# Low halves of the mixer's weight blocks: accumulating transfers in place of VectorE subtractions

## The chip, the core and the metric

The kernel runs on one core of a Trainium2 chip. The core has a matrix engine (TensorE), a vector engine (VectorE), a scalar engine (ScalarE) and a general engine (GpSimd), which work in parallel, each through its own queue of instructions in order; SyncE only issues transfers here. In the profile they are PE (its weight loads PEld), DVE, ACT, POOL and SP. Sixteen DMA engines carry the transfers. The metric is the time of the whole program on the device, in microseconds (us).

## The reference

A decoder trunk of two layers over 512 tokens of width 1024, in float32. Each layer is a feed-forward part, a mixer and a second feed-forward part, each added to x. The mixer, cut to what matters:

```python
h = rms_norm(x, mix_norm[l])
proj = h @ w_in[l]                       # 1024 -> 2048: q, k, v, u of 512 each
q = apply_rope(q, cos, sin)              # 4 heads, two maps of 64 columns each
k = apply_rope(k, cos, sin)
o = diff_attention(q, k, v, lam)         # (softmax(Q1K1) - lam softmax(Q2K2)) V, causal
o = rms_norm(o, subln_gain[l]) * (1.0 - lam_init)
p = pool_mixer(u, pool_w[l], pool_scale[l])   # windows 2, 4, 8, 16, then a linear map
x = x + jnp.concatenate([o, p], axis=-1) @ w_out[l]
```

The feed-forward parts are `x + 0.5 * swiglu(h, w_gate, w_up, w_down)` with 2816 hidden columns.

## The kernel before, in words

**Three products for one.** TensorE multiplies in a rounded float32 form (fp32r in the profile). To keep float32 accuracy each operand is split into a high half, the rounded value, and a low half, the rest, and `mm3` issues three matmuls into one sum: high by high (L95), a second with the weights' high half (L96), and one with the weights' low half (L97). In the profile whi and wlo are the weights' halves. A block's first two products can start when whi is there; the third waits for wlo.

**How weights come in.** All weights are cut into blocks of 128 partitions by up to 1024 columns, 512 KB of float32. The lists `raws` and `plan`, filled before the work starts, hold them in the order of use. `block(src, by_dma)` (L102) adds a block and says how its halves are made. `weights()` hands out the next block, and first prepares blocks up to 4 ahead (`AHEAD`); their raw float32 form, wraw, is loaded by SyncE up to 3 blocks further ahead (`AHEAD_RAW`). There are 6 buffers for wraw and 5 each for whi and wlo, used in turn, so preparing a block also waits until the block five before it has been used for the last time.

**Two ways to make the halves.** Without `by_dma`, `split` copies wraw into whi on ScalarE (L143), which rounds it, and VectorE subtracts whi from wraw into wlo (L144). With `by_dma`, ScalarE writes minus wraw, rounded, into wlo (L164), GpSimd issues a transfer that reads the block from HBM a second time and adds it onto wlo (L165), and ScalarE copies wraw into whi (L166). Before the change the mixer's blocks go the first way; of the feed-forward parts, the gate and up blocks that are used as they are go the second.

**The mixer** (`mix`, L534) uses 26 blocks per layer: query and key projections of four heads, with the v projection (which holds 4 blocks at once), the two u projections and the pooling maps (a block of 256 columns each) among them, and the output projection. The attention of a head runs in four steps (`scores` L607, `turn` L632, `attend` L645) laid among those projections by tables (`S_AT`, `Y_AT`) and lags in counts of work items (`LAG_Q` and others). Scores need a head's qs, ks and kf (the queries' and keys' halves, L571 to L576); GpSimd clears half of kf first (L571).

**The output projection** (`out_work`, L730) has two halves. For its first four blocks it goes over the inner dimension in five stages, as the heads come ready, with all four blocks held from the first stage to the last; then the other four blocks, one after the other, each with all 24 matmuls at once (ps_wo in the profile). Below, out block 4 is the first of these, out block 5 the second. Each finished block is added to x, from which ScalarE and GpSimd start the next norm's sum of squares (ssum).

**Order.** A scheduler lays down the order on each engine ahead of time from a priority and its own estimate of times, so the order on every engine can change when operations are replaced.

Of the kernel before, what the change touches and what calls it, by code (L numbers as in the profile page):

```python
# [70 lines left out]
def trunk(ctx: ExitStack, tc: tile.TileContext, xT, gu1, dn1, win_qk, win_v, win_u, poolw, wout, gu2, dn2, small, lams, consts, outT):  # L71
# [30 lines left out]
    def block(src, by_dma=False):  # L102

        raws.append(src)
        plan.append(("block", len(raws) - 1, by_dma))

    def pair(gu):

        r = len(raws)
        raws.extend(gu[b] for b in (A11, A12, A21, A22))  # L110
        plan.append(("block", r, True))
        plan.append(("block", r + 1, True))
        plan.extend((("sums", r + 3), ("sum", "u1", r), ("sum", "u3", r), ("sum", "u4", r)))
        plan.append(("block", r + 3, True))

    def plain_pairs(first):
        return 2 if first else 1

    for l in range(L):
        for gu, dn in ((gu1, dn1), (gu2, dn2)):  # L120
            if gu is gu2:
                for c in range(2):
                    for i in range(2):
                        block(win_qk[l, c][:, i * 1024 : (i + 1) * 1024])
                for c in range(2):
                    for i in range(2):
                        block(win_v[l, c][:, i * 1024 : (i + 1) * 1024])
                for w in (win_qk[l, 2], win_u[l, 1], win_qk[l, 3], poolw[l, 1], win_u[l, 0], wout[l, 0], wout[l, 1], poolw[l, 0], wout[l, 2], wout[l, 3]):
                    for o in range(0, w.shape[-1], 1024):
                        block(w[:, o : min(o + 1024, w.shape[-1])])  # L130
            for hf, (q0, nq) in enumerate(PARTS):
                for q in range(q0, q0 + nq):
                    if q < plain_pairs(gu is gu1 and l == 0):
                        for b in range(4):
                            block(gu[l, q, b], bool(q or l or gu is gu2))
                    else:
                        pair(gu[l, q])
                for n in range(KD):
                    block(dn[hf][l, n])
# [808 lines left out]
```

## Time and profile before

| | us |
|---|---|
| median of three runs | 1763.78 |
| these runs | 1763.78, 1764.39, 1762.21 |
| profiled execution | 1762.4 |
| its span in the trace | 1760.4 |
| TensorE busy | 1729.1 (98%) |
| weight loads of TensorE busy | 1565.8 (89%) |
| VectorE busy | 1137.3 (65%) |
| ScalarE busy | 946.5 (54%) |
| GpSimd busy | 208.3 (12%) |

The span runs from the first to the last instruction of the trace; the execution's own time is 2.0 us longer. The mean granted clock of TensorE is 0.995 of full speed. The transfers move 240.66 MB, 137 GB/s on the mean: 169.18 MB in SyncE's queue (31.0% of the 16 engines' time) and 69.74 MB in GpSimd's (22.3%). The first mixer lies between about 358 and 530 us of the span, the second between 1227 and 1400 us. A busy share is a mean over the run; whether an engine holds up another is seen only in the waits and the timeline of a stretch. In a timeline a row gives the start, the duration, the line, the operation, and its output and inputs by the program's names; a bracket at its end gives the idle time of the engine before it and what ended that.

### The profile page before, as it was taken

To read this page: it belongs to the slowest core of one execution; us is meant where nothing else is said; L and a number is where in the kernel's file an instruction comes from. 1 tells how busy PE (TensorE), PEld (TensorE's weight loads), DVE (VectorE), ACT (ScalarE), POOL (GpSimd) and SP (SyncE) were. 2 spreads that over 40 slices of the span, in tenths; PEclk is the share of its full clock that TensorE was granted. 3 is DMA by queue.
4 is the path that set the end of the run, shared out by engine and by line. 5 is a ranking of instruction groups with operands and counts; after the bars stand their busy time and mean duration, and the time that the engine had idled before them with its cause. 6 is when DMAs were issued, how large, how long until landed. Compare 5 with 4: busy or idle time off the path is not lost.

```text
span 1760.4 us, 26873 instructions
## 1 busy us (share of the span) xinstructions
PE 1729.1 (98%) x10936; PEld 1565.8 (89%) x10936; DVE 1137.3 (65%) x1507; ACT 946.5 (54%) x1294; POOL 208.3 (12%) x215
## 2 busy tenths in 40 slices
PE   9999999999999999999999999999999999999997
PEld 7889989888788989989889899898887889899996
DVE  6855646577967746646587465466789596466463
ACT  7635626555566626626556265364555665374463
POOL 1001001120021001001210010012100400010001
PEclk9999999999999999999999999999999999999998
DMA  9555746522235747737757377374122647375551
GB/s 287 138 146 149 190 106 159 153 75 75 72 100 134 189 105 168 192 88 170 182 118 196 86 181 183 96 171 146 43 86 61 155 109 203 96 183 165 120 144 48
DMA packets 71723, 240.66 MB, mean 137 GB/s; under 512 B 7856, under 2 KB 12592, under 8 KB 71600
## 3 DMA queue, kind: packets, MB, share of 16 engines
q1 hardware_dynamic: 52304, 169.18, 31.0%
q0 software_dynamic: 19152, 69.74, 22.3%
q8 instruction: 85, 1.39, 0.3%
q14 instruction: 38, 0.31, 0.1%
q10 hardware_dynamic: 144, 0.03, 0.0%
HBM read 236.82 MB, written 2.10 MB: 136 GB/s over the span
## 4 chain that ended last, share of the span: by engine, by line
PE 87%; DVE 5%; DMA 3%; issue 2%; ACT 2%; SPq 1%; POOL 0%; POOLq 0%; DVEq 0%; ACTq 0%
PE ps_dn L96 9%; PE ps_dn L95 9%; PE ps_dn L97 9%; PE ps_a L97 8%; PE ps_a L96 8%; PE ps_a L95 8%; PE ps_c L95 4%; PE ps_c L96 4%; PE ps_c L97 4%; DMA wlo<-gu 2%; PE ps_g L97 2%; PE ps_g L95 2%; PE ps_g L96 2%; PE ps_pr L95 2%; PE ps_pr L97 2%
## 5 line engine op out<-in xcount | busy, mean ns | idle before, releaser
L143 ACT CAST whi<-wraw 128x1024 fp32r<-128x1024 f32 (+2 forms) x275 | 273.7, 997 | 417.2 <-PE ps_dn L96 146.4
L144 DVE TENSOR_TENSOR wlo<-wraw,whi 128x1024 fp32r<-128x1024 f32 (+2 forms) x275 | 317.8, 1157 | 110.0 <-ACT whi L143 108.3
L97 PE MATMUL ps_a<-bhi,wlo 128*128 128x256 f32 x1248 | 353.9, 284 | 2.5 <-DMA wlo<-gu 2.4
L95 PE MATMUL ps_a<-bhi,whi 128*128 128x256 f32 x1248 | 353.9, 284 | 0.5 <-ACT whi L166 0.5
L96 PE MATMUL ps_a<-blo,whi 128*128 128x256 f32 x1248 | 354.1, 284 | 0.0
L96 PE MATMUL ps_dn<-hlo,whi 128*128 128x512 f32 (+1 forms) x716 | 276.6, 386 | 0.0
L97 PE MATMUL ps_dn<-hhi,wlo 128*128 128x512 f32 (+1 forms) x716 | 276.1, 386 | 0.0
L95 PE MATMUL ps_dn<-hhi,whi 128*128 128x512 f32 (+1 forms) x716 | 275.7, 386 | 0.0
L165 POOL DMA_DIRECT2D wlo<-gu x133 | 116.0, 874 | 1113.9 <-ACT wlo L164 754.7
L97 PEld LDWEIGHTS ps_a<-bhi,wlo 128*128 128x128 f32 x1248 | 240.1, 192 | 2.9 <-DMA wlo<-gu 2.9
L95 PEld LDWEIGHTS ps_a<-bhi,whi 128*128 128x128 f32 x1248 | 240.0, 192 | 1.5 <-ACT whi L166 0.7
L96 PEld LDWEIGHTS ps_a<-blo,whi 128*128 128x128 f32 x1248 | 240.1, 192 | 0.8
L166 ACT CAST whi<-wraw 128x1024 fp32r<-128x1024 f32 x133 | 139.2, 1048 | 129.9 <-PE ps_dn L96 62.2
L507 DVE SCALAR_TENSOR_TENSOR x<-ps_dn,x 128x512 f32<-128x512 f32 (+1 forms) x98 | 66.7, 680 | 191.8 <-PE ps_dn L97 191.8
L95 PE MATMUL ps_c<-bhi,whi 128*128 128x256 f32 x624 | 176.9, 283 | 5.7 <-ACT bhi L143 5.7
L97 PE MATMUL ps_c<-bhi,wlo 128*128 128x256 f32 x624 | 176.8, 283 | 0.5 <-DVE wlo L144 0.5
L96 PE MATMUL ps_c<-blo,whi 128*128 128x256 f32 x624 | 176.7, 283 | 0.0
L96 PEld LDWEIGHTS ps_dn<-hlo,whi 128*128 128x128 f32 x716 | 134.5, 188 | 27.8 <-DVE hlo L144 1.4
L97 PEld LDWEIGHTS ps_dn<-hhi,wlo 128*128 128x128 f32 x716 | 134.5, 188 | 27.0
L95 PEld LDWEIGHTS ps_dn<-hhi,whi 128*128 128x128 f32 x716 | 134.5, 188 | 26.8
L164 ACT ACTIVATE wlo<-wraw 128x1024 fp32r<-128x1024 f32 x133 | 140.5, 1057 | 0.2 <-DMA wraw<-gu 0.2
L95 PEld LDWEIGHTS ps_c<-bhi,whi 128*128 128x128 f32 x624 | 119.9, 192 | 6.3 <-ACT bhi L143 6.3
(171 smaller groups left out, 3236.7 us busy)
## 6 DMA issues: line engine op xcount, KB each, us to landing
wraw<-gu SPq DMA_DIRECT2D x174, 512.0 KB, 3.7
wlo<-gu POOLq DMA_DIRECT2D x133, 512.0 KB, 7.2
wraw<-dn SPq DMA_DIRECT2D x64, 512.0 KB, 4.4
wraw<-dn SPq DMA_DIRECT2D x32, 384.0 KB, 3.3
wraw<-wqk SPq DMA_DIRECT2D x16, 512.0 KB, 3.7
wraw<-wo SPq DMA_DIRECT2D x16, 512.0 KB, 3.7
wraw<-wv SPq DMA_DIRECT2D x8, 512.0 KB, 3.6
wraw<-wu SPq DMA_DIRECT2D x8, 512.0 KB, 3.7
```

Of the source, the lines that this page charges most:

```text
L95: nc.tensor.matmul(out, a_hi, b_hi, start=start, stop=False, skip_group_check=more)
L96: nc.tensor.matmul(out, a_hi, b_lo, start=False, stop=False, skip_group_check=more)
L97: nc.tensor.matmul(out, a_lo, b_hi, start=False, stop=stop, skip_group_check=more)
L143: nc.scalar.copy(hi, raw)
L144: nc.vector.tensor_sub(lo, raw, hi.bitcast(F32))
L164: nc.scalar.mul(lo[:, :n], raw[:, :n], -1.0)
L165: nc.gpsimd.dma_start(lo[:, :n], src, accum_op=ALU.add)
L166: nc.scalar.copy(hi[:, :n], raw[:, :n])
L507: nc.vector.scalar_tensor_tensor(x[:, n, ts], ps[:, ts], -0.5, x[:, n, ts], ALU.mult, ALU.add)
```

## The change

The blocks of the mixer's weights are now added with `by_dma`:

```diff
@@ -121,13 +121,13 @@
             if gu is gu2:
                 for c in range(2):
                     for i in range(2):
-                        block(win_qk[l, c][:, i * 1024 : (i + 1) * 1024])
+                        block(win_qk[l, c][:, i * 1024 : (i + 1) * 1024], True)
                 for c in range(2):
                     for i in range(2):
-                        block(win_v[l, c][:, i * 1024 : (i + 1) * 1024])
+                        block(win_v[l, c][:, i * 1024 : (i + 1) * 1024], True)
                 for w in (win_qk[l, 2], win_u[l, 1], win_qk[l, 3], poolw[l, 1], win_u[l, 0], wout[l, 0], wout[l, 1], poolw[l, 0], wout[l, 2], wout[l, 3]):
                     for o in range(0, w.shape[-1], 1024):
-                        block(w[:, o : min(o + 1024, w.shape[-1])])
+                        block(w[:, o : min(o + 1024, w.shape[-1])], True)
```

So each of the mixer's 52 blocks (26 per layer) loses its subtraction on VectorE (L144) and gains a pass on ScalarE (L164) and a transfer issued by GpSimd (L165); its high half is made by L166 in place of L143. VectorE goes from 1353 rows of the program to 1299, ScalarE from 1093 to 1153, GpSimd from 67 to 119. TensorE and SyncE have the same instructions as before; TensorE's order differs in three places of each mixer.

On TensorE, the attention of the first mixer's third head, before (ps_o the attention products, ps_t the transposes of the weights a, ps_pr a projection):

```order
L653 MATMUL ps_o<-v,at 128x256
L95 MATMUL ps_pr<-xhi,whi 128x512
L96 MATMUL ps_pr<-xlo,whi 128x512
L97 MATMUL ps_pr<-xhi,wlo 128x512
L95 MATMUL ps_pr<-xhi,whi 128x512
L96 MATMUL ps_pr<-xlo,whi 128x512
L97 MATMUL ps_pr<-xhi,wlo 128x512
L638 MATMUL ps_t<-ident_r,a 128x128 x2
L654 MATMUL ps_o<-v,at 128x128
```

and now:

```order
L653 MATMUL ps_o<-v,at 128x256
L654 MATMUL ps_o<-v,at 128x128
L638 MATMUL ps_t<-ident_r,a 128x128 x2
L95 MATMUL ps_pr<-xhi,whi 128x512
L96 MATMUL ps_pr<-xlo,whi 128x512
L97 MATMUL ps_pr<-xhi,wlo 128x512
```

The second product (L654) and the two transposes (L638) now stand directly behind the first product, ahead of the six projection matmuls.

On ScalarE, the end of the first mixer before, where the high halves of the last blocks are copied (cath is the output projection's input, xhi the next norm's high half):

```order
L661 ACTIVATE junk,osum<-o,rl 128x128 x2
L676 ACTIVATE cath<-ps_ot,subg_3489 128x512
L143 CAST whi<-wraw 128x1024 x3
L240 ACTIVATE xhi<-x,sm 128x512
L245 ACTIVATE ssum<-x 128x512
```

and now:

```order
L676 ACTIVATE cath<-ps_ot,subg_3493 128x512
L166 CAST whi<-wraw 128x1024
L164 ACTIVATE wlo<-wraw 128x1024 x2
L166 CAST whi<-wraw 128x1024
L164 ACTIVATE wlo<-wraw 128x1024
L166 CAST whi<-wraw 128x1024
L240 ACTIVATE xhi<-x,sm 128x512
L245 ACTIVATE ssum<-x 128x512
```

Three copies in a row have become three copies and three negations, ahead of the next norm's work.

On GpSimd, the same mixer from the clearing of kf to its end, before:

```order
L571 MEMSET kf 64x512 x6
L298 TENSOR_TENSOR rT<-ms,nhalf 128x4 x2
L571 MEMSET kf 64x512 x2
L298 TENSOR_TENSOR rT<-ms,nhalf 128x4 x2
L251 TENSOR_TENSOR ssum<-ssum,sq 128x512
```

and now, from the last u projection's blocks on (wo are the output projection's blocks, pw a pooling map):

```order
L165 DMA wlo<-wu 128x1024
L571 MEMSET kf 64x512 x2
L298 TENSOR_TENSOR rT<-ms,nhalf 128x4 x2
L165 DMA wlo<-wu 128x1024
L165 DMA wlo<-wo 128x1024 x4
L571 MEMSET kf 64x512 x2
L165 DMA wlo<-pw 128x256
L298 TENSOR_TENSOR rT<-ms,nhalf 128x4
L165 DMA wlo<-wo 128x1024
L298 TENSOR_TENSOR rT<-ms,nhalf 128x4
L165 DMA wlo<-wo 128x1024 x3
```

The clearing of the last head's kf (L571) now stands behind five transfers, and the small operations of the head norms (L298) between transfers of wo.

## Rows read from the trace of the kernel before

**Rows 1.** Windows, the stretches of the mixers. Columns: us, then per engine; PEclk, DMA share, GB/s.
```profile
400.00:500.00 100.00, 95.50 (x502) 80.01 (x501) 84.97 (x190) 55.68 (x135) 5.10 (x7) 1.00 0.23 70
1300.00:1400.00 100.00, 96.07 (x474) 79.57 (x473) 80.53 (x163) 58.81 (x119) 17.06 (x16) 0.98 0.32 85
```

**Rows 2.** Waits of TensorE, whole run. Columns: us in total, times, longest us.
```profile
PE ps_c L95 <- ACT bhi L143: 5.7, 3, 1.9
PE ps_s L617 <- DVE qs L576: 5.0, 6, 1.2
PE ps_a L97 <- DMA wlo<-gu: 2.4, 1, 2.4
...
PE ps_t L638 <- DVE a L629: 2.0, 2, 1.0
...
PE ps_s L617 <- ACT p L621: 1.1, 3, 0.5
...
PE ps_o L654 <- DVE at L642: 0.4, 2, 0.2
```

**Rows 3.** Line L144. Columns: count: ns min/median/max, first to last start; forms.
```profile
L144 DVE TENSOR_TENSOR wlo<-wraw,whi x275: 406/1224/1237, 5.4 to 1727.0; 128x1024 fp32r<-128x1024 f32 x116, 128x768 fp32r<-128x768 f32 x16, 128x256 fp32r<-128x256 f32 x6
```

**Rows 4.** Timeline of VectorE, 446 to 455 us. Columns: start us, duration us.
```profile
446.92 1.21 DVE L144 TENSOR_TENSOR wlo<-wraw,whi 128x1024 fp32r<-128x1024 f32 x1
448.04 0.17 DVE L690 COPY win<-win 128x8 f32<-128x8 f32 x1
...
453.87 0.48 DVE L629 SCALAR_TENSOR_TENSOR a<-p,ratio 128x256 f32<-128x256 f32 x1
454.26 0.29 DVE L642 TENSOR_TENSOR at<-ps_t,at 128x128 fp32r<-128x128 f32 x1
```

**Rows 5.** Timeline of TensorE, 452 to 457 us.
```profile
452.85 0.33 PE L653 MATMUL ps_o<-v,at 128*128 128x256 f32 x1
...
454.50 0.41 PE L638 MATMUL ps_t<-ident_r,a 128*128 128x128 f32 x2
...
456.24 0.28 PE L653 MATMUL ps_o<-v,at 128*128 128x256 f32 x1
```

**Rows 6.** Timeline of ScalarE, 463 to 476 us.
```profile
472.51 0.63 ACT L575 ACTIVATE qs<-t 64x512 fp32r<-64x512 f32 x1
```

**Rows 7.** Timeline of TensorE, 469 to 475 us; brackets: idle before, releaser.
```profile
474.55 0.30 PE L617 MATMUL ps_s<-kf,qs 128*128 128x128 f32 x1 [1.21 <-DVE qs L576]
```

**Rows 8.** Timeline of ScalarE, 524 to 527 us.
```profile
525.29 1.05 ACT L164 ACTIVATE wlo<-wraw 128x1024 fp32r<-128x1024 f32 x1
```

**Rows 9.** Line L165, whole run.
```profile
L165 POOL DMA_DIRECT2D wlo<-gu x133: 849/872/1210, 21.0 to 1702.2; - x133
...
DMA to landing us min/median/max: 5.2/7.2/15.5
```

**Rows 10.** Timeline of ScalarE, 489 to 516 us.
```profile
507.49 2.95 ACT L143 CAST whi<-wraw 128x1024 fp32r<-128x1024 f32 x3 [1.51 <-PE ps_wo L96]
```

**Rows 11.** Timeline of TensorE, 507 to 514 us.
```profile
507.29 0.39 PE L97 MATMUL ps_wo<-cath,wlo 128*128 128x512 f32 x1
...
513.89 0.39 PE L97 MATMUL ps_wo<-cath,wlo 128*128 128x512 f32 x1
```

**Rows 12.** Timeline of GpSimd, 524 to 528 us.
```profile
526.64 0.87 POOL L165 DMA_DIRECT2D wlo<-gu  x1 [1.82 <-ACT wlo L164]
```

**Rows 13.** Line L165, from 508 to 545 us.
```profile
DMA to landing us min/median/max: 5.8/8.6/10.2
```

**Rows 14.** Windows, three short stretches.
```profile
558.00:568.00 10.00, 8.11 (x54) 7.79 (x53) 9.61 (x10) 8.17 (x11) 0.86 (x1) 0.83 0.44 132
908.00:918.00 10.00, 8.11 (x67) 7.82 (x66) 10.00 (x10) 9.55 (x13) 1.72 (x2) 1.00 0.46 130
1342.00:1349.00 7.00, 5.82 (x25) 5.13 (x26) 6.64 (x19) 3.41 (x13) 0.00 (x0) 0.76 0.27 81
```

**Rows 15.** Timeline of GpSimd, 415 to 505 us.
```profile
459.28 1.10 POOL L571 MEMSET kf<- 64x512 f32 x2 [15.35 <-PE ps_y L97]
```

## The prediction

> **What bounds the kernel now.** TensorE. Read first the stretches that hold the two mixers: TensorE is busy 95.5 and 96.1 of 100 us there, VectorE 85 and 81, ScalarE only 56 and 59 [rows 1]. VectorE is nowhere in the run as full as here, and one of its jobs is the subtraction that this change removes. Read next who makes TensorE wait [rows 2]: four of the rows belong to the mixers alone (ps_s, ps_t and ps_o are attention tiles): 5.0 us for the queries' low half (DVE L576), 2.0 for the attention weights (DVE L629), 1.1 for the exponentials (ACT L621) and 0.4 for their low half (DVE L642), together 8.5 us in two mixers. That is all the visible waiting that a relieved VectorE can give back; a TensorE that never waits gains nothing from a faster VectorE. The remaining rows of that view are the reverse case: one wait of 2.4 us for exactly the kind of transfer that the change adds, and 5.7 us in feed-forward code that stays as it is.
>
> **What is removed.** 26 blocks per mixer, 52 in all, lose one subtraction of about 1.22 us [rows 3] (four of the 52 have 256 columns and cost 0.4), some 60 us of VectorE. Nearly all lies under matmuls. Where it does not, the timeline of the first mixer shows it: two subtractions, one at 446.92 and its like 13 us earlier, stand in VectorE's queue just ahead of the operands that TensorE waits for [rows 4]. Each frees about 1.1 us, the distance from its start to the next instruction (446.92 to 448.04). So up to 449 us VectorE gets some 2.3 us earlier (two such, rounded up) and the waits before that point close.
>
> How much stays? The program now also asks for operands earlier. In the new order TensorE's second attention product (L654) and two transposes (L638) stand directly behind the first product instead of behind six projection matmuls more. In the trace the first product starts at 452.85 and those transposes at 454.50 [rows 5], just after their operands: weights a at 453.87 for 0.48, the low half at 454.26 for 0.29 [rows 4]. With TensorE some 2.5 us earlier it asks at 450.4; VectorE, 2.3 us earlier, delivers at 454.55 - 2.3 = 452.2. It waits 1.8 us. Twelve projection matmuls of 0.23 us follow (six of them and the first product fill 452.85 to 454.50), so the next product starts near 455.1; before it started 12 matmuls and the transposes after 452.85, at 456.24 by the same spacing. Of 2.5 us, 1.2 are left there. The next waits, for the last head's queries, are set by ScalarE as much as by VectorE: its last scaled query copy starts at 472.51 [rows 6] and TensorE resumes at 474.55 [rows 7]. ScalarE now has two 1.05 us passes per block here where it had one, so it moves up less than VectorE; I get about 2 us for the whole mixer. I take half of the 8.5 us, **4.2 us gained in two mixers**; the ends are 0 (all taken by ScalarE and the new order) and 8.5.
>
> **What is added.** Per block one ScalarE negation, 1.05 us [rows 8], one GpSimd issue of 0.87 us and a transfer that lands 5.2, 7.2 or 15.5 us (least, median, most) after its issue starts [rows 9]. ScalarE's 27 us per mixer fit into its 41 to 44% of idle time. GpSimd is 5 to 17% busy in these stretches [rows 1]. The transfers re-read 48 blocks of 512 KB and four small ones; DMA is 23 to 32% busy there [rows 1]. What counts is latency. A low half was ready about 2.3 us after its buffer came free (copy, subtraction); now it takes copy 1.05 + negation 1.05 + 0.3 to the issue + 7.2, about 9.6 us. Five buffers turn, so most blocks have three other blocks, some 17 us, in between, and nothing waits. I went through the 26 and one has no cover: out block 5. Four blocks are held by the output projection's first half until its last stage, and out block 5 takes the first of them; only out block 4, 24 matmuls, stands between.
>
> In the trace its copy starts at 507.49, when that buffer is released [rows 10]; the low half's release is the matmul that starts at 507.29, and the first use of the new low half starts at 513.89 [rows 11]. Now: copy to 508.44, negation to 509.49, 0.3 us to the issue (negation 525.29 + 1.05, issue 526.64 [rows 8, 12]), so issue at 509.8. The landing decides. Transfers of this kind just behind it took 5.8 to 10.2, median 8.6 us [rows 13]; over the run the median is 7.2 [rows 9]. Three raw loads and two more accumulating transfers start within 4 us of it, so I take 7.9, between the two. It lands at 517.7, 3.8 us after 513.89. The other queues move with it: the two blocks behind have 5.5 us more each and that wait besides. **7.6 us lost in two mixers**. Ends: 5.2 us gives 1.1 each, 2.2 in all; 10.2 gives 6.1 each, 12.2.
>
> The Trainium skill, page "DMA: Bandwidth & Descriptors", section "Anatomy of one DMA — SWDGE (gpsimd) path", fits a GpSimd transfer as 2.0 us plus bytes over 436 GB/s. By it 512 KB would be an estimated 3.2 us and land at 513.0, ahead of 513.89: no wait, and the change would gain. No run row agrees: the fastest of 133 took 5.2 [rows 9], so I keep the rows; the case in which it comes near is the first rival.
>
> **The clock.** In two stretches the granted clock sank (0.83 over 10 us, 0.76 over 7 us [rows 14]). The lower level is half the speed (1.2 for 2.4 GHz), so each cost 10 x 0.17 or 7 x 0.24, 1.7 us. Just before the first TensorE had waited for bhi, 1.9 us at most in one piece [rows 2]; before the second it had waited in the attention of the second mixer. At 908 us it came out of a like wait for bhi and the clock stayed at 1.00 [rows 14]. A wait of 3.8 us is longer than any of these: I price half a fall for each, 1.7 us lost in all. The fall at 1342 us follows mixer waits that shrink: half of 1.7, 0.85, gained.
>
> **Sum.** -4.2 + 7.6 + 1.7 - 0.85 = +4.2 us. Against the profiled execution, 1762.4 us (span 1760.4 and 2.0 around it), 1766.6. That execution is 1.4 below the median of 1763.78, so against the median **1768.0 us**.
>
> Hidden at no cost: one GpSimd issue (0.87 us) that now stands before the last ssum addition at each mixer's start, under the squares that this addition waits for (uncovered, up to 0.9 per mixer); and the transfers of the other 25 blocks, under the matmuls of the blocks in between.
>
> **Rivals.**
> 1. Faster: the landing at out block 5 takes 5.2 to 6 us, since DMA before 508 us was nearly idle, and VectorE's relief keeps its full 8.5 us. Then -8.5 - 1.7 + 2 x 1.5 = -7.2: 1756.6 us. For it: light places land in 5.2. Against: ScalarE's chain before 472.51, the new order, and the raw loads beside it. It decides below a wait of about 2 us per mixer. Chance 0.18 (with half the effect it gives 1759 to 1760).
> 2. No change: half the gain, landing near 6.5, a wait of 2.4 each and no fall of the clock: -4.2 - 0.85 + 4.8 = -0.3, 1763.5 us; up to 3.5 us either way. Chance 0.30.
> 3. Slower still: GpSimd works in order, and the clearing of the last head's kf (459.28 before [rows 15]) now stands behind four wo transfers, the last of which needs a ScalarE negation that I put some 6 us ahead of the last scaled query copy [rows 6]. If ScalarE is far later than I think, the clearing ends after that copy and the scores wait: 2 to 3 us per mixer on top, 1773 us. Chance 0.07.
> My forecast: 0.45.
>
> A difference under about 0.2%, 3.5 us, can't be told from none here. Faster 0.18, same 0.30, slower 0.52. Range 1760 to 1774: it leaves out most of rival 1 and the worst of rival 3. The likeliest case alone spans 1767 to 1772.
>
> **What would show it.** Right: the waits view has a new row, TensorE's ps_wo (L97) for the wlo transfer of wo, 2 times, 3 to 4 us each; the rows for L576, L629 and L642 shrink to about half; VectorE's 85% falls to about 70, ScalarE's 56 rises to about 70; transfers of wo near 510 us land in 7 to 9 us. Wrong: no such row; mixer waits gone entirely or unchanged; a wait on kf or on ssum in its place.

## The result and the profile after

The changed kernel takes 1775.47 us (median of four runs, 1771.53 to 1776.95) against 1764.09 for the kernel before (1762.21 to 1765.04): a ratio of 1.0067, interval 1.0053 to 1.008, 11.4 us slower. The direction and the main wait were forecast; 1775.47 lies 1.5 us above the range, and 7.5 above the value given. The profiled execution of after took 1776.23 us, 13.8 more than that of before. By the pages of the profile VectorE has 52 instructions fewer (1507 to 1455), and ScalarE (1294 to 1346) and GpSimd (215 to 267) 52 more each, one for each block.

The waits of TensorE in the changed kernel, whole run (us in total, times, longest), answer to [rows 2]:

```profile
PE ps_wo L97 <- DMA wlo<-wo: 7.3, 2, 4.1
...
PE ps_s L617 <- DVE qs L576: 4.6, 6, 1.2
...
PE ps_s L617 <- ACT p L621: 1.5, 4, 0.5
PE ps_o L654 <- DVE at L642: 1.5, 2, 0.8
...
PE ps_o L653 <- ACT at L641: 1.4, 2, 0.7
...
PE ps_v L96 <- DMA wlo<-wv: 0.9, 1, 0.9
```

The first row is new and is the forecast one: two times, 7.3 us together (forecast 7.6). The wait for a (L629) is gone, as expected. But the other attention rows did not shrink: 4.6 + 1.5 + 1.5 + 1.4 = 9.0 us, where before the four rows made 8.5. A wait for the copy of at on ScalarE (L641) is new, and that for its low half (L642) has grown from 0.4 to 1.5. The last row is one I had priced at nothing: the v projection waits 0.9 us for a low half. There the weights are the second operand of `mm3`, so their low half is read by the second product already (L96), not by the third.

The windows of both mixers answer to [rows 1], those of 6 to 10 us behind them to [rows 14]:

```profile
400.00:500.00 100.00, 95.55 (x503) 80.32 (x502) 72.12 (x176) 67.11 (x150) 18.01 (x22) 1.00 0.59 136
1310.00:1410.00 100.00, 92.23 (x453) 76.04 (x453) 65.10 (x148) 65.75 (x128) 26.73 (x28) 0.98 0.57 132
517.00:523.00 6.00, 5.54 (x14) 4.39 (x15) 1.53 (x1) 5.08 (x7) 5.56 (x5) 0.54 1.06 281
890.00:896.00 6.00, 5.92 (x25) 4.94 (x26) 1.72 (x3) 0.75 (x1) 1.94 (x3) 0.72 0.69 110
915.00:925.00 10.00, 8.11 (x54) 7.82 (x53) 9.45 (x9) 8.04 (x10) 0.86 (x1) 0.83 0.46 126
1391.00:1401.00 10.00, 6.76 (x24) 5.09 (x23) 5.11 (x5) 9.41 (x14) 7.69 (x7) 0.83 1.05 243
1441.00:1451.00 10.00, 8.11 (x54) 7.80 (x53) 9.45 (x10) 8.03 (x11) 0.87 (x1) 0.83 0.44 127
```

VectorE fell from 85 to 72 us of 100 and ScalarE rose from 56 to 67, close to the forecast of about 70 for both. TensorE stayed at 95.55 (95.50 before): VectorE was relieved and TensorE did not notice. (The second window holds the second wait for out block 5, so its 92.23 can't be set beside the 96.07 of before.) DMA in the mixer went from 0.23 to 0.59 of the engines, 136 GB/s in place of 70.

The chain at out block 5 of the first mixer, on ScalarE (start, duration), then GpSimd, then TensorE, then the landing of that one transfer:

```profile
506.83 1.05 ACT L166 CAST whi<-wraw 128x1024 fp32r<-128x1024 f32 x1 [1.50 <-PE ps_wo L96]
507.79 2.01 ACT L164 ACTIVATE wlo<-wraw 128x1024 fp32r<-128x1024 f32 x2
```

```profile
509.15 1.82 POOL L165 DMA_DIRECT2D wlo<-wo  x2 [8.11 <-ACT wlo L164]
```

```profile
512.98 0.39 PE L96 MATMUL ps_wo<-catl,whi 128*128 128x512 f32 x1
517.46 0.80 PE L97 MATMUL ps_wo<-cath,wlo 128*128 128x512 f32 x1 [4.09 <-DMA wlo<-wo]
518.05 0.63 PE L95 MATMUL ps_wo<-cath,whi 128*128 128x512 f32 x1
```

```profile
DMA to landing us min/median/max: 8.3/8.3/8.3
```

Copy at 506.83, negation at 507.79, issue at 509.15, landing 8.3 us later at 517.4; TensorE, which had started its last matmul at 512.98, resumes at 517.46. Forecast were an issue at 509.8 and a landing at 517.7; the issue came 0.6 us sooner, the landing took 0.4 us longer, and TensorE stood at the matmul 0.5 us sooner (513.37 against 513.89), so these errors partly cancel. The matmul behind the wait takes 0.63 us in place of the 0.39 of [rows 11]: the engine comes back at the lower clock.

### The profile page after: what moved, and what is told of

Same layout as the page of the kernel before. It is cut to its first block, busy times and chain, and to the rows that moved or that the text cites. A ratio compares the mean times of both kernels' runs of the same rounds, so it can differ in the third digit from the quotient of the medians.

```text
span 1774.5 us, 26987 instructions
## 1 busy us (share of the span) xinstructions
PE 1735.3 (98%) x10936; PEld 1570.6 (89%) x10936; DVE 1083.0 (61%) x1455; ACT 991.0 (56%) x1346; POOL 247.3 (14%) x267
## 4 chain that ended last, share of the span: by engine, by line
PE 83%; issue 5%; DMA 5%; DVE 4%; ACT 3%; POOL 1%; POOLq 0%; SPq 0%; DVEq 0%; ACTq 0%
PE ps_dn L96 9%; PE ps_dn L95 9%; PE ps_dn L97 9%; PE ps_a L97 8%; PE ps_a L96 8%; PE ps_a L95 8%; PE ps_c L95 4%; PE ps_c L96 4%; PE ps_c L97 4%; DMA wlo<-gu 3%; PE ps_g L97 2%; PE ps_g L96 2%; PE ps_g L95 2%; PE ps_pr L95 2%; PE ps_pr L97 2%
## 5 line engine op out<-in xcount | busy, mean ns | idle before, releaser
L143 ACT CAST whi<-wraw 128x1024 fp32r<-128x1024 f32 (+2 forms) x223 | 222.0, 996 | 364.6 <-PE ps_dn L96 146.4
L96 PE MATMUL ps_a<-blo,whi 128*128 128x256 f32 x1248 | 354.9, 284 | 0.0
L144 DVE TENSOR_TENSOR wlo<-wraw,whi 128x1024 fp32r<-128x1024 f32 (+2 forms) x223 | 257.5, 1155 | 104.5 <-ACT whi L143 103.6
L166 ACT CAST whi<-wraw 128x1024 fp32r<-128x1024 f32 (+1 forms) x185 | 191.2, 1034 | 166.6 <-issue 60.6
L96 PE MATMUL ps_dn<-hlo,whi 128*128 128x512 f32 (+1 forms) x716 | 276.6, 386 | 0.0
L165 POOL DMA_DIRECT2D wlo<-gu x133 | 116.7, 882 | 1116.0 <-ACT wlo L164 728.3
L96 PEld LDWEIGHTS ps_a<-blo,whi 128*128 128x128 f32 x1248 | 241.0, 193 | 0.8
L164 ACT ACTIVATE wlo<-wraw 128x1024 fp32r<-128x1024 f32 (+1 forms) x185 | 192.6, 1042 | 1.2 <-PE ps_v L96 0.9
L96 PE MATMUL ps_c<-blo,whi 128*128 128x256 f32 x624 | 176.6, 283 | 0.0
L96 PEld LDWEIGHTS ps_dn<-hlo,whi 128*128 128x128 f32 x716 | 134.6, 188 | 27.8 <-DVE hlo L144 1.4
```

Source lines behind the costliest of these rows:

```text
L96: nc.tensor.matmul(out, a_hi, b_lo, start=False, stop=False, skip_group_check=more)
L143: nc.scalar.copy(hi, raw)
L144: nc.vector.tensor_sub(lo, raw, hi.bitcast(F32))
L164: nc.scalar.mul(lo[:, :n], raw[:, :n], -1.0)
L165: nc.gpsimd.dma_start(lo[:, :n], src, accum_op=ALU.add)
L166: nc.scalar.copy(hi[:, :n], raw[:, :n])
```

## The experiments

Ratios are against the kernel before on the same chip, with 95% intervals. Line numbers of some kernels are shifted by up to six where lines were added.

**Is the loss out block 5, or the traffic?** Two kernels undo the change for a few blocks.

```diff
+ late = wout[l, 2], wout[l, 3]              # out blocks 4 to 7
- block(w[:, o : ...], True)
+ block(w[:, o : ...], w is not late[0] and w is not late[1])
```

> The last four blocks of each mixer (out blocks 4 to 7) go back to the copy and the subtraction; the other 22 keep the accumulating transfer. Theory A: the loss of 11 us is the wait of TensorE for out block 5's low half (7.3 us in two mixers) with the falls of the granted clock behind it (about 1.7 us each), while the relief of VectorE gave nothing. Then the waits for wlo<-wo are gone and the time is 1764 us, within 2 of before. Theory B: the loss is spread, from twice the traffic in the mixers. Then only a part comes back, 1769 to 1772 us.

Measured 1761.66 us, ratio 0.9993 [0.9982, 1.0004]: the whole loss is gone while 22 of 26 blocks per mixer still come by transfer. Theory A; B falls. It also shows what those 22 are worth in this order: nothing measurable. TensorE's order in this trace is that of the changed kernel, matmul for matmul, so the order is not what made the loss.

```diff
+ late = wout[l, 2]
- block(w[:, o : ...], True)
+ block(w[:, o : ...], not (w is late and o))   # out block 5 alone
```

> Of the changed kernel, out block 5 alone goes back to the copy and the subtraction (one block of each mixer). Theory A1: it is the only block without cover, so the waits for wlo<-wo go: 1762 to 1766 us. Rival A2: out block 6 stood in the shade of that wait; its low half landed at 521.2 us, and without the wait it is asked for near 518.7. Then a wait of 1 to 3 us per mixer stays, and the time is 1766 to 1771 us.

Measured 1764.44 us, ratio 1.0013 [1.0002, 1.0024]. Two rows of its waits:

```profile
PE ps_pl L96 <- DVE xlo L242: 0.7, 1, 0.7
...
PE ps_wo L97 <- DMA wlo<-wo: 0.2, 1, 0.2
```

The wait for wo shrinks from 7.3 to 0.2 us, so A1 holds and A2 does not. One block per mixer carried the loss; the split takes away both its transfer and its negation on ScalarE, which the next two kernels take apart. What stays above the kernel with four blocks split is small; the wait for xlo, of the norm behind the mixer, is part of it.

**Landing, or ScalarE's extra passes?** Both kernels here have TensorE's order of the changed kernel too.

```diff
- nc.scalar.mul(lo[:, :n], raw[:, :n], -1.0)        # for out blocks 4 to 7
+ nc.vector.tensor_scalar_mul(lo[:, :n], raw[:, :n], -1.0)
```

> As the changed kernel, but the negations of out blocks 4 to 7 run on VectorE, which is idle there, in place of ScalarE. This takes the burst of three negations between three copies off ScalarE and leaves the transfers. If the landing is what counts (theory A), out block 5's transfer starts about 1 us earlier and the wait shrinks from 4.1 to about 3 us: 1770 to 1774 us. If ScalarE's burst is what counts (rival E: it delays the next norm), nearly all comes back: 1762 to 1766 us.

Measured 1775.03 us, ratio 1.0063 [1.0047, 1.0079]: nothing comes back, so rival E falls for this kernel. (Theory A's 1770 to 1774 us was 1 us short.) The wait and the landings of the three transfers issued near 507 us, from a profiled execution of 1769.44 us, the fastest of the six:

```profile
PE ps_wo L97 <- DMA wlo<-wo: 6.6, 2, 3.9
```

```profile
DMA to landing us min/median/max: 9.2/12.1/15.3
```

```profile
506.75 2.82 POOL L169 DMA_DIRECT2D wlo<-wo  x3 [7.04 <-DVE wlo L166]
```

The three now follow each other without a gap, 2.82 us from 506.75 on, and land after 9.2, 12.1 and 15.3 us. In the changed kernel the first landed after 8.3, with the third issued only at 511.98. The wait is 6.6 in place of 7.3 us. TensorE too stands 1.3 us earlier in this execution (511.69 against 512.98 for its last matmul), so the issue is some 1.1 us earlier against its use, and 0.9 of that went into the longer landing, with the other two issued right behind it.

The negation's own price:

```diff
- nc.gpsimd.dma_start(lo[:, :n], src, accum_op=ALU.add)   # left out for the mixer's blocks
```

> The mixer's blocks get the negation on ScalarE as their low half, without the transfer that would add the block onto it, so the low half's value is left out. Against the kernel without low halves this is the price of 52 negations on ScalarE alone. Theory A: under 3 us more than that kernel, 1761 to 1765 us, with no wait for a wo block. Rival C: 5 to 8 us more than it, 1760 to 1764 us, with waits for the copies of the attention weights (at, L641) and for qs.

Measured 1770.68 us, ratio 1.0043 [1.0027, 1.0059], 11.5 us above the kernel without low halves below, where I expected 3 at most under theory A and 8 under rival C. Neither had the right place:

```profile
PE ps_ms L295 <- POOL ssum L257: 3.6, 3, 1.2
...
PE ps_pl L96 <- DVE xlo L247: 1.8, 3, 1.2
```

Most of the price is paid behind the mixers. Three negations between three copies push the next norm's first xhi copy from 510.34 us in the kernel before to 512.84, and the feed-forward part waits for xlo and ssum there. In the changed kernel the wait for out block 5 lies over this delay; I had counted the last blocks' passes as free. The profiled executions (1770.84 us, and 1758.89 without low halves) are 12.0 us apart. The two rows above make 5.0 of it (5.4 against 0.4 us there), and the granted clock 5.1: it is 0.83 over 10 us four times here (from 538, 886, 913 and 1435 us) and once there (from 70).

Against the kernel before beside it (1762.35 us) this one is 8.3 us slower without any second transfer, and the kernel with the negations on VectorE is as slow as the changed one without these passes on ScalarE. So two causes lie over one another at the end of each mixer, and each is enough for most of the loss; the changed kernel pays the landing.

**An earlier buffer.**

```diff
- raw = wpool.tile([P, WSLOT], F32, name="wraw", bufs=6)
+ raw = wpool.tile([P, WSLOT], F32, name="wraw", bufs=5)
- lo = wpool.tile([P, WSLOT], F32R, name="wlo", bufs=5)
+ lo = wpool.tile([P, WSLOT], F32R, name="wlo", bufs=6)
```

> As the changed kernel, with six buffers for low halves in place of five and five for raw blocks in place of six. Theory A: out block 5's low half then finds a buffer that is free long before the first four blocks are released, its transfer starts early, and the wait of 7.3 us and the clock's falls behind it go, with the traffic left as it is: 1764 to 1766 us. Theory B (traffic): no change, 1773 to 1777 us. One raw buffer less may cost a little in the feed-forward parts in either case (up to 3 us).

Measured 1785.44 us, ratio 1.0128 [1.0107, 1.0149]. Its waits have no row for wo, so the sixth buffer did remove that wait; but these stand in its place:

```profile
PE ps_ms L289 <- POOL ssum L251: 11.2, 2, 5.6
...
PE ps_c L95 <- DVE u L433: 4.9, 1, 4.9
```

Both theories miss the time. The 11.2 us for the norm's sum behind the two mixers are no price of the sixth buffer as far as the trace shows. VectorE stands 7.6 us for a raw load of the feed-forward part (in the changed kernel the longest such wait is 4.1), and the addition to x of which the sum is made stands behind the two additions that need the load:

```profile
541.87 1.23 DVE L175 TENSOR_TENSOR wsum<-wraw 128x1024 f32<-128x1024 f32 x1 [7.62 <-DMA wraw<-gu]
543.13 1.22 DVE L176 TENSOR_TENSOR wraw<-wraw 128x1024 f32<-128x1024 f32 x1
544.27 0.68 DVE L752 TENSOR_TENSOR x<-ps_wo,x 128x512 f32<-128x512 f32 x1
```

That points to the missing raw buffer. What a sixth low buffer would give by itself was not run.

**What can VectorE's relief give at most?**

```diff
- nc.scalar.mul(lo[:, :n], raw[:, :n], -1.0)
- nc.gpsimd.dma_start(lo[:, :n], src, accum_op=ALU.add)
  nc.scalar.copy(hi[:, :n], raw[:, :n])
+ lo = hi
```

> The mixer's 52 blocks get no low half at all: the third product reads the high half instead, so that part of the result is left out. VectorE has neither subtraction, ScalarE its one copy as before, no second transfer: the most that relieving VectorE alone can give. Theory A (the attention's waits hang on a chain through ScalarE and the order, not on VectorE's load): 1 to 4 us below before, 1760 to 1763 us. Rival C (they hang on VectorE, and the negations on ScalarE gave the gain away): the whole 8.5 us, about 1755 us.

Measured 1759.14 us, ratio 0.9981 [0.9968, 0.9995]: 3.3 us, by the interval 0.9 to 5.6, with no subtraction, no negation and no transfer. Its attention waits:

```profile
PE ps_s L623 <- DVE qs L582: 4.8, 6, 1.2
PE ps_o L660 <- DVE at L648: 2.1, 4, 0.8
...
PE ps_o L659 <- ACT at L647: 1.3, 2, 0.7
```

4.8 + 2.1 + 1.3 = 8.2 us, against 8.5 before. So with this table the 8.5 us were not VectorE's subtractions' to give back, and of these waits ScalarE's negations explain at most the 0.8 us between 8.2 and 9.0 (rival C falls). Of the 3.5 us between the profiled executions of before and of this kernel these rows make 0.3, and one fall of the clock fewer makes 1.7.

**Other engines for the halves.** Both with the last four blocks split.

```diff
- nc.scalar.copy(hi[:, :n], raw[:, :n])
+ nc.vector.tensor_copy(hi[:, :n], raw[:, :n])            # both
- nc.scalar.mul(lo[:, :n], raw[:, :n], -1.0)
+ nc.gpsimd.tensor_scalar_mul(lo[:, :n], raw[:, :n], -1.0)   # the second only
```

> The last four blocks split as before the change; for the other 22 the low half comes by transfer, with the negation on ScalarE and the copy for the high half on VectorE. So ScalarE has as many passes as before the change, and VectorE a copy in place of a subtraction, at a price that no trace has shown (0.6 to 1.2 us). If ScalarE's second pass is what held the gain back: 1757 to 1760 us. If not: 1760 to 1764 us, as with both on ScalarE.

> As the kernel before it, with the negations of the 22 blocks on GpSimd: ScalarE makes none of their halves. If the attention's waits hang on ScalarE, 1753 to 1758 us; if on the chain's latency and the order of the queues, 1758 to 1763 us. Against it: GpSimd's pass has no price yet, and the clearing of kf and the norms' small operations stand behind it in order; if a pass takes over 3 us, waits for kf or rT appear and the time is over 1765 us.

The first took 1762.83 us, ratio 0.9997 [0.9987, 1.0007], no gain; the second 1806.55, ratio 1.025 [1.0234, 1.0266], the slowest of all. The copy on VectorE in the first and in the second, then GpSimd's passes (count: ns min/median/max):

```profile
L168 DVE CAST whi<-wraw x44: 286/694/1179, 341.5 to 1345.5; 128x1024 fp32r<-128x1024 f32 x40, 128x256 fp32r<-128x256 f32 x4
```

```profile
L171 DVE CAST whi<-wraw x44: 294/1103/5094, 341.2 to 1384.4; 128x1024 fp32r<-128x1024 f32 x40, 128x256 fp32r<-128x256 f32 x4
```

```profile
L166 POOL TENSOR_SCALAR wlo<-wraw x44: 842/3072/4018, 341.5 to 1383.9; 128x1024 fp32r<-128x1024 f32 x40, 128x256 fp32r<-128x256 f32 x4
```

GpSimd needs 3.07 us for a pass that ScalarE does in 1.05, and VectorE's copy takes 1.10 us in the median and up to 5.09, where it took 0.69 and at most 1.18 without GpSimd's passes. The waits that grew are not those for kf or rT, as expected for this case, but those for qs (13.8 us) and the weights a (6.7).

**Who sets the attention's waits: load or order?** First the keys' second copy moved from ScalarE to VectorE, on three bases (the first and third with the last four blocks split, the third with the 22 negations on VectorE too).

```diff
- nc.scalar.copy(ks[other, c, :], t[own, 1, :])
+ nc.vector.tensor_copy(ks[other, c, :], t[own, 1, :])
```

> The kernel with the last four blocks split, and one of the two copies per half of the keys (ks, L573 of before) moved from ScalarE to VectorE, which that kernel has relieved. Theory A: the attention's waits for qs hang on ScalarE, whose six passes in a row (4 us for kf, ks and qs) stand behind the copy of a weight block that waits for its buffer; with two of the six gone, qs comes about 1.3 us earlier and the waits for qs (4.6 us) fall to about half: 1758 to 1760 us, 2 to 3 below before. Rival C (VectorE): 16 more passes on VectorE make it no faster, 1761 to 1765 us.

> The kernel before, with the same copy of the keys moved to VectorE, the subtractions kept. Here VectorE is 85% busy in the stretch. Theory A: qs hangs on ScalarE, so it gains too, 1 to 2 us: 1761 to 1762. Rival C: VectorE is the bound, so its 16 more passes cost 2 to 5 us: 1765 to 1768 us.

> As the first of these three, with the negations of the 22 blocks on VectorE as well (0.69 us each there by the kernel with the last four so, against 1.05 on ScalarE). ScalarE then has as many block passes as before and two fewer per half of the keys. Theory A: the fastest of the three, 1756 to 1759 us. Rival C: slower than the first, 1761 to 1765 us.

Measured 1761.71 (0.9993 [0.9984, 1.0002]), 1766.35 (1.0024 [1.0013, 1.0035]) and 1768.15 us (1.0025 [1.0015, 1.0036]). Theory A as I put it, that ScalarE's passes set the waits, falls: with ScalarE relieved the waits for qs are 5.2 us, where they were 4.6. With the subtractions kept, 16 more passes on VectorE cost 3.5 us, so its queue does count there. The third kernel, which should have been the fastest, is the slowest, with 3.0 us of waits for low halves of the v projection among its rows. In the first kernel ScalarE has both qs ready by 435.83, but VectorE gets to the second low half, behind the rest of its own order, only here:

```profile
434.55 1.28 ACT L576 ACTIVATE qs<-t 64x512 fp32r<-64x512 f32 x2
```

```profile
438.42 0.42 DVE L574 CAST ks<-t 64x512 fp32r<-64x512 f32 x1
438.86 0.69 DVE L575 TENSOR_TENSOR ks<-t,kf 64x512 fp32r<-64x512 f32 x1
439.58 0.69 DVE L577 SCALAR_TENSOR_TENSOR qs<-t,qs 64x512 fp32r<-64x512 f32 x1
```

```profile
440.41 0.30 PE L618 MATMUL ps_s<-kf,qs 128*128 128x128 f32 x1 [1.36 <-DVE qs L577]
```

Then TensorE's asking time was moved instead: the third head's first two scores one work item later (k1), the last head's too (k2), and both tables on the kernel before (k3, k4).

```diff
- S_AT = ((3, 4, 6, 8), (10, 11, 13, 15), (19, 20, 23, 25), (26, 26, 28, 29))
+ S_AT = ((3, 4, 6, 8), (10, 11, 13, 15), (20, 21, 23, 25), (26, 26, 28, 29))   # k1, k3
+ S_AT = ((3, 4, 6, 8), (10, 11, 13, 15), (20, 21, 23, 25), (27, 27, 28, 29))   # k2, k4
```

> The kernel with the last four blocks split, and in the table S_AT the third head's first two scores one work item later (20, 21 in place of 19, 20; four products, about 2.8 us of matmuls). If the wait for that head's qs (1.2 us in each mixer, with the excess 1.4) comes from when TensorE asks, in the given order (theory F), it goes, and the time falls by 1 to 3 us, to 1759 to 1761 us. If operands come later as TensorE asks later, or the next waits grow by as much, nothing is gained: 1761 to 1764 us.

> As the kernel before it, with the last head's first two scores one work item later too (27, 27 in place of 26, 26). Theory F: the two waits for the last head's qs (0.3 and 0.8 us per mixer) go as well, another 1 to 2 us: 1757 to 1760 us. Against it: the last head then stands closer to the output projection, whose stages need it; then waits for exponentials or weights of that head take their place: 1761 to 1766 us.

> The kernel before, with the third head's first two scores one work item later as in the first of these. If the order alone sets these waits (theory F), it gains what that one gains against its own base, 1 to 3 us: 1760 to 1762 us. If VectorE's load does (rival C), the wait moves on behind the subtractions and nothing is gained: 1762 to 1765 us.

> The kernel before with the whole table of the fastest one (third head's first scores at 20, 21, the last head's at 27, 27), subtractions kept. If that table alone makes the gain of 5 us, about 1758 us. If it needs the relieved VectorE, as the third head's part did (2 us slower without it): 1762 to 1766 us.

| ratio to the kernel before | subtractions (before) | transfers, last four blocks split |
|---|---|---|
| table as it was | 1 | 0.9993 [0.9982, 1.0004] |
| third head later | 1.0013 [1.0004, 1.0023] | 0.9983 [0.9972, 0.9994] |
| third and last head later | 1.0000 [0.9988, 1.0012] | 0.9967 [0.9955, 0.9979] |

The runs of the first row were on another chip than those below it. The transfers with the last table took 1757.57 us against 1762.86 for the kernel before beside it; the interval also lies clear of that in the first row. Neither half does it alone. In each of the two lower rows TensorE's order is the same in both kernels, matmul for matmul, so the difference within a row is what the transfers give in one order: 4.8 us with the third head later (1760.05 against 1764.81 on the same chip). In the first row the scheduler changed TensorE's order with the transfers, as shown ahead of the prediction, and no run has the old order with the relief. The attention waits of the fastest kernel, then those of the same table with subtractions:

```profile
PE ps_s L618 <- DVE qs L577: 1.9, 2, 0.9
PE ps_o L654 <- ACT at L642: 1.8, 2, 0.9
...
PE ps_t L639 <- DVE a L630: 1.2, 4, 0.3
...
PE ps_y L95 <- DVE o L660: 1.0, 2, 0.5
```

```profile
PE ps_t L638 <- DVE a L629: 6.7, 4, 1.9
...
PE ps_y L95 <- DVE o L659: 1.2, 2, 0.6
...
PE ps_o L654 <- DVE at L642: 0.4, 2, 0.2
```

1.9 + 1.8 + 1.2 + 1.0 = 5.9 us with transfers; 6.7 + 1.2 + 0.4 = 8.3 with subtractions, most of it for the weights a, which VectorE makes. These two executions took nearly the same time (1759.89 us, the slowest of eight, and 1759.49, the fastest of twelve), so the rows show where each kernel waits, and only the medians show the gain. In the later order VectorE's load counts and its relief is worth something; with the table as it was, the same relief only moves the waits.

## Why the prediction was wrong, point by point

**The new wait: right.** Out block 5 waits for its transfer, twice, 7.3 us against 7.6, by the chain as it was worked out; undoing that one block removes it. That the sum is so close is partly luck: the two waits are 4.1 and 3.2 us, and the errors of the first one's terms partly cancel.

**The relief of VectorE: the step that failed.** The prediction took half of the mixer's 8.5 us, 4.2 us, as gained. The waits came to 9.0, a loss of 0.5; with 22 blocks by transfer and no new wait the gain is 0.7 us by the medians, with an interval from -0.7 to 3.2, and even with no low halves at all it is 3.3. I read "TensorE waits for VectorE" as "VectorE is overloaded". That row says only which operand came last. TensorE asks earlier when a wait ahead is removed, and VectorE's operand comes from a chain of small steps in fixed order. The two waits that took the place of the one removed show it, on TensorE and on ScalarE:

```profile
451.94 0.39 PE L653 MATMUL ps_o<-v,at 128*128 128x256 f32 x1 [0.64 <-ACT at L641]
453.08 0.33 PE L654 MATMUL ps_o<-v,at 128*128 128x128 f32 x1 [0.75 <-DVE at L642]
```

```profile
450.11 1.04 ACT L166 CAST whi<-wraw 128x1024 fp32r<-128x1024 f32 x1
451.04 0.69 ACT L676 ACTIVATE cath<-ps_ot,subg 128x512 fp32r<-128x512 f32 x1
451.62 0.27 ACT L641 CAST at<-ps_t 128x128 fp32r<-128x128 f32 x1
```

The copy of at (451.62) stands behind a block's copy and a cath pass on ScalarE. TensorE, early by one removed wait, asks for the product at 451.3 (451.94 - 0.64), 1.5 us sooner than it ran in [rows 5], and stands 0.64 us there and 0.75 for the low half. The prediction had seen that pair of products and expected 1.2 of 2.5 us to survive; nothing did: behind the pair TensorE starts the next product at 456.25 us, in before at 456.24.

That VectorE's load does count in another order is shown by the two pairs of kernels with a later table: there the same relief is worth 4.8 us (third head later) and 0.33% (both later). Whether the waits stayed here because of the table or because of the order that the scheduler laid down with the change is open, since no run separates these.

**The clock: mis-sized.** I priced half a fall for each new wait, 1.7 us, less 0.85 for one that would go. The first new wait brought more than a whole fall, 0.54 over 6 us (2.8), the second a whole one, 0.83 over 10 us (1.7). The fall at 1342 us did go. But there are also falls at 890, 915 and 1441 us, 1.7 each, where before had one, at 558 [rows 14]. Together after loses 9.6 us to them and before 3.4: 6.2 us more where the sum had 0.85. The falls at 915 and 1441 follow the wait for bhi that stands there in both kernels and is followed by a fall in one execution and not in another; the one at 890 follows a wait for ssum that grew from 0.7 to 1.2 us; the kernel with VectorE's copies (1762.83 us) has a wait of 1.2 us there too, and no fall. Why these three came in this execution was not settled. By the sum, either of the two errors alone, 4.7 us on the relief or 5.4 on the clock, would have left the time inside the range (1772.7 or 1773.4 us).

**The other blocks: nearly right.** Twenty-four of the 25 show no wait in the changed kernel; a block of the v projection, four of which are held at once, cost 0.9 us once. ScalarE's passes for the last blocks were put at nothing too, without a look at what stands behind them. They cost nothing here only because the wait for out block 5 lies over them.

**The sum again**, for the profiled executions: 7.3 (out block 5) + 6.2 (clock) + 0.9 (v) + 0.5 (attention) = 14.9, against 13.8 measured; the rest is small waits of either sign. The rivals: the faster one needed both an early landing and the whole relief, and had neither; no change needed a landing near 6.5 us and no fall of the clock, and the landing took 8.3; the fourth head's kf was not late, no row names it.

## What to carry to other kernels

A transfer that replaces a computation trades an engine's time for latency: look for the one buffer that is released shortly before its next use, and leave only that block on the short path. An engine named in a wait is not shown to be overloaded by it; the test is to take its load away, and then to move the asking time. Here relief and order had to be changed together; with the table as it was, the relief showed no gain.

## What the runs showed of the hardware

VectorE slowed beside an engine that was meant to take work off the others. In the kernel with negations on GpSimd, two copies on VectorE and GpSimd's work around them:

```profile
341.19 0.69 DVE L171 CAST whi<-wraw 128x1024 fp32r<-128x1024 f32 x1 [1.54 <-PE ps_dn L96]
...
345.27 5.09 DVE L171 CAST whi<-wraw 128x1024 fp32r<-128x1024 f32 x1 [1.24 <-PE ps_dn L96]
```

```profile
341.47 3.05 POOL L166 TENSOR_SCALAR wlo<-wraw 128x1024 fp32r<-128x1024 f32 x1 [0.68 <-PE ps_dn L97]
...
345.48 1.58 POOL L258 TENSOR_TENSOR ssum<-ssum,sq 128x512 f32<-128x512 f32 x1
346.74 3.07 POOL L166 TENSOR_SCALAR wlo<-wraw 128x1024 fp32r<-128x1024 f32 x1
```

The first copy starts 0.28 us ahead of a GpSimd pass and takes 0.69 us, as without such passes. The second starts 0.21 us ahead of GpSimd's addition of ssum, behind which the next pass follows, and ends at 350.36, just behind that pass, which ends at 349.81. The Trainium skill, page "Perfetto Trace Analysis", section "Optimizing Scalar/DVE Operations", says that the two engines share a read port of the local memory, which a VectorE operation that uses two ports holds as an exclusive lock, so that moving work between them might not help. The trace agrees in the outcome: the median copy took 1.10 us in place of 0.69, the longest 5.09 in place of 1.18, and the kernel is 2.5% slower. That the port is the cause is not shown by it.

A copy of 128x1024 to the rounded form takes 0.69 us on VectorE, where the subtraction of the same size takes 1.22 and ScalarE's copy 1.05. And accumulating transfers of 512 KB that are issued one behind the other land later and later, 9.2, 12.1 and 15.3 us after their issues. In the kernel before, the plain loads of the same 512 KB in SyncE's queue (wraw of gu) land 3.7 us after their issue in the median, the accumulating ones (wlo of gu) 7.2. In the changed kernel the plain loads slowed where the new transfers run: those of wo take 7.9 us in the median in place of 3.7.
